# One common set of four PSUM banks for scores and transposes, in place of two private pairs, in a two-layer decoder trunk

## The chip, the core and the metric

The kernel runs on one core of a Trainium2 chip. The metric is the device time of one execution in microseconds (us), the median of several runs. Five engines work side by side, each through its own queue in order: TensorE (PE, matmuls and transposes; PEld is its weight load), VectorE (DVE), ScalarE (ACT), GpSimd (POOL) and SyncE (SP), which issues most DMA transfers. PE writes its results to PSUM, eight banks of 128 partitions by 512 fp32 values; DVE and ACT read them out from there.

## The reference, cut to what matters

x is 512 tokens by 1024 features, fp32. Layer 0 mixes tokens by stick-breaking heads and differential heads, layer 1 by dilated heads; each layer then has a squared-ReLU MLP (1024 to 4096 and back) and a gated embedding.

```python
for i in range(DEPTH):                       # DEPTH = 2
    hn = rmsnorm(h, norm_mix_g[i])
    h = h + (even_mixer if i % 2 == 0 else odd_mixer)(hn, ...)
    hn = rmsnorm(h, norm_mlp_g[i])
    u = square(relu(hn @ w_mlp_up[i]))
    h = h + u @ w_mlp_down[i]
    gate = sigmoid(rmsnorm(h, norm_ple_g[i]) @ w_ple_gate[i])
    h = h + (p[i] @ w_ple_proj[i]) * gate
return rmsnorm(h, final_norm_g)

# differential heads:  prob = softmax(scale * q.k + bias);  attn = prob[0] - lam * prob[1];  o = attn @ v
# stick-breaking:      z = scale * q.k;  w = exp(log_sigmoid(z) + sum of log_keep over later keys);  o = w @ v
# dilated:             three causal branches (window, stride), combined by their softmax denominators
```

## The kernel before, in words

**Precision.** Every fp32 operand of a large matmul is split into a high part (`hi`, `wh`, `uh`, by an ACT copy, L119 for weights, L168 for activations) and a low part (`lo`, `wl`, `ul`, by a subtraction, L120 on DVE or POOL for weights, L169 on DVE). A product is three matmuls: L128, L129 and L130 in the trace.

**Stages.** A layer is: statistics of its norm, the mixer with its projections, the output projection, the MLP, the gate. In the mixer the heads are taken in four groups; layer 0 takes groups 2 and 3 (differential) and then 0 and 1 (stick-breaking), layer 1 four dilated groups. `project` makes values, queries and keys of one group; while it runs for group g+1, `attend` handles group g, in steps interleaved with it. A step computes the scores of one 128-token block (L460, L461), lets DVE and ACT make weights of them (L475 and L478, L479 for softmax; L536, L539 for stick-breaking), and three steps later transposes the weights on PE (L486), after which ACT and DVE copy them out as a high and a low part (L490, L491); two steps later they multiply the values (L501).

**Norm.** `finish` sums squares over partitions with two matmuls (L236, L237); rsqrt on ACT and DVE follows (L192 to L198). `tok_cols` transposes the result into token columns with four transposes (L259), which wait for the last DVE step, L198; L261 reads them out, and the evacuation of values (L397, L398) needs them. `prepare` (layer 0 alone) makes the bias rows with two small matmuls (L315) and reads them out on DVE (L317).

**The last gate.** `ple_final` makes the gate token by token: eight groups of four transposes of the stream h (L707), each copied out by DVE (L708), beside the split of the gate's weights (L119, L120) and the gate's matmuls.

**PSUM.** `ps(tag)` draws a bank of a tag. Before, there are three banks "mm" for projection accumulators, two "sc" for scores (and `prepare`), two "tp" for transposes (and for norm sums, `tok_cols` and `ple_final`) and one "pv". `ps_wide` walks round all eight for wide stages: the projection of a layer's first group, the MLP, the gate.

**What sets the order.** The kernel is written in a framework whose scheduler orders each engine's instructions by the data they need and the engines' queues. One rule of it matters here, as the orders below show it: the tiles of one tag get their banks in the order of the program, that is, of each tile's first writer. A tile of one tag can be started ahead of an earlier tile of another tag, never ahead of one of its own. A tile's first writer waits until the reader of the tile that held the bank before has read it.

Of the kernel before, what the change touches and what calls it, by code (L numbers as in the profile page):

```python
# [61 lines left out]
def trunk(  # L62
# [8 lines left out]
    def nm(s):  # L71
        uid[0] += 1
        return f"{s}_{uid[0]}"
# [8 lines left out]
    def const(shape, name, dtype=F32):  # L82
        return cpool.tile(shape, dtype, tag=name, name=name)
# [3 lines left out]
    def t2k(tag, pool=None, dtype=F32):  # L87
        return (pool or spool).tile([P, S], dtype, tag=tag, name=nm(tag), bufs=T_BUFS.get(tag, 2))
# [1 line left out]
    def col(name="c"):  # L90
        return spool.tile([P, 1], F32, tag="col", name=nm(name), bufs=24)

    PS_BUFS = {"mm": 3, "sc": 2, "tp": 2, "pv": 1}

    def ps(tag):
        return psum.tile([P, S], F32, tag=tag, name=nm(tag), bufs=PS_BUFS[tag])

    wide = ["mm", "mm", "mm", "sc", "sc", "tp", "tp", "pv"]
    wide_i = [0]

    def ps_wide():
# [89 lines left out]
    def rsqrt(y, t, mean, eps, eps_t, scale=1.0, tables=None):  # L191
        ln = nc.scalar.activation(y, mean, AF.Ln, bias=eps_t, scale=scale)  # L192
        if tables is not None:
            order(ln.ins, tables)
        nc.scalar.activation(y, y, AF.Exp, scale=-0.5)
        nc.vector.tensor_tensor(t, y, y, op=ALU.mult)
        nc.vector.scalar_tensor_tensor(t, mean, eps / scale, t, op0=ALU.add, op1=ALU.mult)
        nc.vector.scalar_tensor_tensor(y, t, 3.0 / scale, y, op0=ALU.subtract, op1=ALU.mult)  # L198
# [13 lines left out]
    class Norm:  # L212
# [16 lines left out]
                nc.vector.tensor_tensor(self.acc, self.acc, sq, op=ALU.add)  # L229

        def finish(self, tables=None):
            mp = ps("tp")
            hi, lo = t2k("e", dtype=F32R), t2k("e", dtype=F32R)
            nc.scalar.activation(hi, self.acc, AF.Copy)
            nc.vector.tensor_tensor(lo, self.acc, hi.bitcast(F32), op=ALU.subtract)
            nc.tensor.matmul(mp, ones_r, hi, start=True, stop=False)  # L236
            nc.tensor.matmul(mp, ones_r, lo, start=False, stop=True)  # L237
            rsqrt(self.acc, t2k("e"), mp, NORM_EPS, eps_n, tables=tables)
            return self.acc
# [14 lines left out]
            newton(dst, x, t)  # L254

    def tok_cols(rstd):
        rp = ps("tp")
        for t in range(QT):
            nc.tensor.transpose(rp[:, t * P:(t + 1) * P], rstd[:, t * P:(t + 1) * P], ident)  # L259
        rc = spool.tile([P, QT], F32, tag="rcol", name=nm("rcol"), bufs=2)  # L260
        nc.vector.tensor_scalar(rc, rp.rearrange("p (t c) -> p t c", c=P)[:, :, 0], -0.5, None, op0=ALU.mult)  # L261
        return rc
# [37 lines left out]
    def prepare():  # L300
        a, b, c, d = (t2k("e") for _ in range(4))
        lamt = t2k("tmp")[:, 0:4 * HD].rearrange("p (j c) -> p j c", j=4)
        nc.sync.dma_start(d[0:32, 384:400], t5_table)
        nc.sync.dma_start(a[0:32], onehot[:, 0:512])
        nc.sync.dma_start(d[0:32, 0:128], onehot[:, 512:640])
        for l, m in enumerate((b, c)):
            nc.sync.dma_start(m[0:16], bass.AP(tensor=offs.tensor, offset=offs.offset + l * UL, ap=[[0, 16], [1, 512]]))
        nc.sync.dma_start(
            d[0:16, 128:384].rearrange("p (l c) -> p l c", l=2),
            bass.AP(tensor=offs.tensor, offset=offs.offset + 512, ap=[[0, 16], [UL, 2], [1, 128]]))  # L310
        nc.sync.dma_start(lamt, bass.AP(tensor=lambdas.tensor, offset=lambdas.offset, ap=[[0, P], [HD, 4], [1, HD]]))
        for c0, src, offm in ((0, a[0:32], (b[0:16], c[0:16])),
                              (512, d[0:32, 0:128], (d[0:16, 128:256], d[0:16, 256:384]))):
            up = ps("sc")[0:16, 0:src.shape[-1]]
            nc.tensor.matmul(up, d[0:32, 384:400], src, start=True, stop=True)  # L315
            for l in range(2):
                nc.vector.scalar_tensor_tensor(offm[l], up, -1.0, offm[l], op0=ALU.mult, op1=ALU.add)  # L317
                nc.sync.dma_start(urow[l, :, c0:c0 + src.shape[-1]], offm[l])
        nc.vector.tensor_tensor(lamt[:, 0:2, :], lamt[:, 0:2, :], lamt[:, 2:4, :], op=ALU.mult)
        lsum = const([P, 2], "lsum")  # L320
        nc.vector.reduce_sum(lsum, lamt[:, 0:2, :], axis=AX.X)
        nc.scalar.activation(lsum, lsum, AF.Exp)
        nc.vector.tensor_tensor(neglam, lsum[:, 1:2], lsum[:, 0:1], op=ALU.subtract)
        nc.vector.tensor_scalar(neglam, neglam, -LAMBDA_INIT, None, op0=ALU.add)
        nc.vector.tensor_scalar(gsub, gcols[:, 48:49], -0.5 * (D // P) * (1.0 - LAMBDA_INIT), None, op0=ALU.mult)
# [10 lines left out]
    def mixer(layer, norm, nxt):  # L336
        st = ExitStack()
# [11 lines left out]
        def statistics():  # L349
            if not layer:  # L350
                for k in range(KT):
                    norm.stats(k, last_split)
            stat["rstd"] = norm.finish(use_tables(sig_tail) if layer else None)
            stat["rcol"] = tok_cols(stat["rstd"])
# [100 lines left out]
        def scores(hd, i):  # L455
            q, kh, kl = hd
            n = max(256, P * (i + 1))
            sp = ps("sc")
            qs = slice(i * P, (i + 1) * P)
            nc.tensor.matmul(sp[:, 0:n], q[:, qs], kh[:, 0:n], start=True, stop=False)  # L460
            nc.tensor.matmul(sp[:, 0:n], q[:, qs], kl[:, 0:n], start=False, stop=True)  # L461
            return sp
# [18 lines left out]

        def transpose_in(e, i, pt):
            n = P * (i + 1)
            tp = ps("tp")
            for j in range(i + 1):
                nc.tensor.transpose(tp[:, j * P:(j + 1) * P], e[:, j * P:(j + 1) * P], ident)  # L486
            src = tp[:, 0:n].rearrange("p (j c) -> p j c", c=P)
            dh = pth[pt][:, i:i + 3 * i + 1:3, :]
            dl = ptl[pt][:, i:i + 3 * i + 1:3, :]
            nc.scalar.activation(dh, src, AF.Copy)  # L490
            nc.vector.tensor_tensor(dl, src, dh.bitcast(F32), op=ALU.subtract)  # L491
# [13 lines left out]
        def attend(g, kind, v, heads):  # L505
# [66 lines left out]
            def step(n):  # L572
                if n < QT * nh:
                    ready[n] = weights(n // QT, n % QT)
                m = n - LAG
                if 0 <= m < QT * nh:
                    transpose_in(ready.pop(m), m % QT, pts[m // QT])
                m = n - LAG - PVLAG
                if m >= 0 and m % QT == QT - 1 and m // QT < nh:
                    combine(m // QT)  # L580
                m -= 1
                if kind == "diff" and m >= 0 and m % QT == QT - 1 and m // QT < nh:
                    subnorm(m // QT)
# [17 lines left out]
        if layer == 0:  # L601
            prepare()
# [94 lines left out]
    def ple_final(layer, fpool, pj, norm):  # L697
# [4 lines left out]
        for t in range(QT):  # L702
            ht = fpool.tile([P, D], F32, tag=f"ht{t}", name=nm("ht"), bufs=1)
            for c in range(2):
                tp = ps("tp")
                for k in range(4):
                    nc.tensor.transpose(tp[:, k * P:(k + 1) * P], h[4 * c + k][:, t * P:(t + 1) * P], ident)  # L707
                nc.vector.tensor_copy(ht[:, 512 * c:512 * c + 512], tp)  # L708
            hk.append(ht)
# [13 lines left out]
        for c in range(2):  # L723
# [17 lines left out]
            if c == 0:  # L741
                for b in range(4):
                    for t in range(QT):
                        contract(t, b, 0)
                    if b == 1:
                        rcol = tok_cols(norm.finish())
            for t in range(QT):
# [28 lines left out]
                if t < QT - 2:  # L776
                    finish(*done.pop())
        for t, r in done[::-1]:
            finish(t, r, () if t == QT - 1 else (ex, ad))

    sig_tail = []
    for layer in range(DEPTH):
        n_mlp, n_ple, n_next = Norm(1, layer), Norm(2, layer), Norm(0, layer + 1)
        mixer(layer, norm, n_mlp)
        with tc.tile_pool(name=f"ppool{layer}", bufs=1) as ppool:
            lo_eng[0] = nc.vector
            pj = ple_proj(layer, ppool)
            with tc.tile_pool(name=f"fpool{layer}", bufs=1) as fpool:
                mlp(layer, fpool, n_mlp, n_ple)
            with tc.tile_pool(name=f"gpool{layer}", bufs=1) as gpool:  # L790
                if layer < DEPTH - 1:
                    ple_t(layer, gpool, pj, n_ple, n_next)
                else:
                    ple_final(layer, gpool, pj, n_ple)
        norm = n_next
        lo_eng[0] = nc.gpsimd
# [77 lines left out]
```

## Time and profile before

| | |
|---|---|
| median of 3 runs | 1342.75 us (1341.68 to 1342.84) |
| the profiled execution | 1343.02 us |
| its span in the trace | 1341.2 us, so 1.8 us lie around it |
| instructions | 16293 |
| PE, matmuls on it | 6360 |
| mean granted clock of PE | 0.995 |
| PE idle for L259 to get the norm's result | 3.1 us in two places |

The profile gives busy time per engine, idle time before an instruction and what ended it. A timeline row is: start (us), duration (us), engine, line, operation, out<-in, shape, count; in brackets, when there was idle time ahead of it, how long and what ended it. Matmuls overlap, so a duration is longer than the step to the next: the wide matmuls (512 columns) follow each other at some 0.23 us although each row says 0.39. A window row gives the busy time of the engines in that stretch, then the granted clock of PE (1.00 is full) and the share and rate of the DMA. The prediction shows the rows it uses.

### The profile page before, as it was taken

What the parts mean: (1) busy time and instruction counts of PE and PEld (TensorE: products, weight loads), DVE (VectorE), ACT (ScalarE), POOL (GpSimd) and SP (SyncE); (2) the same over time, 40 slices, a digit from 0 to 9 for tenths busy, and PEclk for the clock granted to TensorE, in tenths of its full rate; (3) what the DMA queues carried; (4) which work ended last, traced back from release to release, by engine and by line L of the source; (5) the groups of instructions that cost most, each with busy time, mean ns of one, the idle gap of its engine ahead of it and who ended that gap; (6) DMA issues with size and microseconds to landing.
All of it is one profiled execution on the core that took longest, in us unless ns stands there. A gap on an engine that the chain in (4) does not pass through costs nothing.

```text
span 1341.2 us, 16293 instructions
## 1 busy us (share of the span) xinstructions
PE 1302.9 (97%) x6360; PEld 1090.5 (81%) x6360; DVE 818.1 (61%) x1397; ACT 633.2 (47%) x1087; POOL 149.0 (11%) x84
## 2 busy tenths in 40 slices
PE   8999988999999999999999999999999999999997
PEld 6878876788888888888879889788888888888886
DVE  6688899765344343445767888977544434434566
ACT  6576766564233232344456667766422313224334
POOL 2222322200000000000013222221000000000001
PEclk9999999999999999999999999999999999999999
DMA  6322101322222223222232222223222222232221
GB/s 218 101 95 70 56 26 48 111 86 103 94 95 94 96 100 106 104 99 94 94 118 79 79 87 79 64 95 110 94 95 95 94 97 100 104 106 96 95 79 64
DMA packets 23453, 124.66 MB, mean 93 GB/s; under 512 B 2832, under 2 KB 3568, under 8 KB 10704
## 3 DMA queue, kind: packets, MB, share of 16 engines
q1 hardware_dynamic: 23376, 123.62, 26.9%
q8 instruction: 50, 0.82, 0.2%
q14 instruction: 27, 0.22, 0.1%
HBM read 121.43 MB, written 2.18 MB: 92 GB/s over the span
## 4 chain that ended last, share of the span: by engine, by line
PE 77%; DVE 14%; ACT 6%; issue 2%; DMA 0%; SPq 0%; ACTq 0%
PE mm L129 12%; PE mm L128 12%; PE mm L130 12%; PE tp L130 5%; PE tp L129 5%; PE tp L128 5%; PE sc L130 5%; PE sc L129 5%; PE sc L128 5%; PE pv L129 3%; PE pv L130 3%; PE pv L128 3%; DVE qq L434 2%; PE pv L501 2%; DVE e L539 1%
## 5 line engine op out<-in xcount | busy, mean ns | idle before, releaser
L119 ACT ACTIVATE wh<-raw 128x1024 fp32r<-128x1024 f32 (+1 forms) x214 | 222.4, 1042 | 504.3 <-PE mm L129 176.9
L128 PE MATMUL mm<-hi,wh 128*128 128x512 f32 x564 | 226.3, 401 | 1.4 <-ACT wh L294 1.3
L120 DVE TENSOR_TENSOR wl<-raw,wh 128x1024 fp32r<-128x1024 f32 x154 | 188.1, 1224 | 59.6 <-ACT wh L119 35.9
L129 PE MATMUL mm<-lo,wh 128*128 128x512 f32 x564 | 220.8, 391 | 0.4 <-DVE lo L169 0.4
L130 PE MATMUL mm<-hi,wl 128*128 128x512 f32 x564 | 220.6, 391 | 0.3 <-DVE wl L120 0.3
L120 POOL TENSOR_TENSOR wl<-raw,wh 128x1024 fp32r<-128x1024 f32 (+1 forms) x60 | 138.3, 2306 | 347.6 <-ACT wh L119 326.2
L130 PEld LDWEIGHTS mm<-hi,wl 128*128 128x128 f32 x564 | 105.9, 188 | 23.2 <-DVE wl L120 0.7
L128 PEld LDWEIGHTS mm<-hi,wh 128*128 128x128 f32 x564 | 106.1, 188 | 21.8 <-ACT wh L294 1.5
L129 PEld LDWEIGHTS mm<-lo,wh 128*128 128x128 f32 x564 | 106.2, 188 | 20.3 <-DVE lo L169 1.1
L478 ACT ACTIVATE e<-e,mn 128x128 f32<-128x128 f32 (+3 forms) x96 | 53.9, 561 | 51.1 <-DVE mn L475 50.6
L128 PE MATMUL mm<-uh,wh 128*128 128x512 f32 x192 | 74.7, 389 | 0.0
L129 PE MATMUL mm<-ul,wh 128*128 128x512 f32 x192 | 74.7, 389 | 0.0
L130 PE MATMUL mm<-uh,wl 128*128 128x512 f32 x192 | 74.7, 389 | 0.0
L130 PE MATMUL sc<-hi,wl 128*128 128x512 f32 x168 | 66.3, 395 | 0.0
L129 PE MATMUL sc<-lo,wh 128*128 128x512 f32 x168 | 65.9, 392 | 0.0
L128 PE MATMUL sc<-hi,wh 128*128 128x512 f32 x168 | 65.8, 392 | 0.0
L128 PE MATMUL mm<-wh,hi 128*128 128x256 f32 (+1 forms) x216 | 65.8, 305 | 0.0
L129 PE MATMUL mm<-wl,hi 128*128 128x256 f32 (+1 forms) x216 | 64.7, 300 | 0.4 <-DVE wl L120 0.4
L130 PE MATMUL mm<-wh,lo 128*128 128x256 f32 (+1 forms) x216 | 64.3, 298 | 0.0
L645 DVE TENSOR_TENSOR h<-h,mm 128x512 f32<-128x512 f32 x24 | 16.5, 687 | 72.7 <-PE mm L130 72.7
L129 PE MATMUL tp<-lo,wh 128*128 128x512 f32 x152 | 59.1, 389 | 0.0
L128 PE MATMUL tp<-hi,wh 128*128 128x512 f32 x152 | 59.1, 389 | 0.0
(265 smaller groups left out, 2837.1 us busy)
## 6 DMA issues: line engine op xcount, KB each, us to landing
raw<-in_w_up_dram SPq DMA_DIRECT2D x32, 1024.0 KB, 4.9
raw<-in_w_down_dram SPq DMA_DIRECT2D x32, 1024.0 KB, 4.9
raw<-in_w_in_dram SPq DMA_DIRECT2D x23, 1024.0 KB, 4.9
raw<-in_w_gate_dram SPq DMA_DIRECT2D x8, 1024.0 KB, 4.8
bias<-urow SPq DMA_DIRECT2D x24, 256.0 KB, 3.2
raw<-in_w_outa_dram SPq DMA_DIRECT2D x8, 768.0 KB, 4.3
h<-in_xT_dram SPq DMA_DIRECT2D x8, 256.0 KB, 5.5
raw<-in_w_outb_dram SPq DMA_DIRECT2D x2, 1024.0 KB, 4.8
```

Source lines behind the costliest of these rows:

```text
L119: nc.scalar.activation(hi, src, AF.Copy)
L120: lo_eng[0].tensor_tensor(lo, src, hi.bitcast(F32), op=ALU.subtract)
L128: nc.tensor.matmul(acc, lh, rh, start=start, stop=False)
L129: nc.tensor.matmul(acc, lh, rl, start=False, stop=False)
L130: nc.tensor.matmul(acc, ll, rh, start=False, stop=stop)
L434: nc.vector.tensor_tensor(q[b], f[a], q[a].bitcast(F32), op=ALU.subtract)
L478: nc.scalar.activation(e[:, 0:n], e[:, 0:n], AF.Exp, scale=-1.0, bias=mn, accum_out=s)
L501: nc.tensor.matmul(op[:, q0:S], stat(j), mov, start=c == 0, stop=c == nmm - 1)
L539: nc.vector.tensor_tensor_scan(kr, kr, kr, 1.0, op0=ALU.mult, op1=ALU.bypass)
L645: nc.vector.tensor_tensor(h[2 * c + i], h[2 * c + i], acc, op=ALU.add)
```

## The change

The tags "sc" and "tp" become one tag, "st", with four banks. The number of banks stays eight, nothing is computed otherwise, and the round of `ps_wide` names the new tag in the same four places. Every tile that was of a pair, of the scores, transposes, norm sums, `tok_cols`, `prepare` and `ple_final`, takes its bank from the common four, in program order.

```diff
-    PS_BUFS = {"mm": 3, "sc": 2, "tp": 2, "pv": 1}
+    PS_BUFS = {"mm": 3, "st": 4, "pv": 1}
...
-    wide = ["mm", "mm", "mm", "sc", "sc", "tp", "tp", "pv"]
+    wide = ["mm", "mm", "mm", "st", "st", "st", "st", "pv"]
...
         def finish(self, tables=None):
-            mp = ps("tp")
+            mp = ps("st")
...
     def tok_cols(rstd):
-        rp = ps("tp")
+        rp = ps("st")
...
-            up = ps("sc")[0:16, 0:src.shape[-1]]
+            up = ps("st")[0:16, 0:src.shape[-1]]
...
-            sp = ps("sc")
+            sp = ps("st")
...
         def transpose_in(e, i, pt):
             n = P * (i + 1)
-            tp = ps("tp")
+            tp = ps("st")
...
             for c in range(2):
-                tp = ps("tp")
+                tp = ps("st")
```

Three places show what the scheduler makes of it. The first is on PE at the start of layer 0: L236 and L237 sum the norm, `sc_264` (now `st_264`) is an accumulator of the second half of the keys, L259 are `tok_cols`' four transposes. Before:

```order
L236 MATMUL tp_312<-e_313,ones_r 128x512
L237 MATMUL tp_312<-e_314,ones_r 128x512
L128 MATMUL sc_264<-hi_130,wh_259 128x512
...
L128 MATMUL sc_264<-hi_162,wh_259 128x512
L129 MATMUL sc_264<-lo_163,wh_259 128x512
L259 MATMUL tp_325<-ident,rstd_289 128x128 x4
L130 MATMUL sc_264<-hi_162,wl_260 128x512
L128 MATMUL sc_264<-hi_166,wh_259 128x512
```

Of the change:

```order
L236 MATMUL st_312<-e_313,ones_r 128x512
L237 MATMUL st_312<-e_314,ones_r 128x512
L259 MATMUL st_325<-ident,rstd_289 128x128 x4
L128 MATMUL st_264<-hi_130,wh_259 128x512
L129 MATMUL st_264<-lo_131,wh_259 128x512
L130 MATMUL st_264<-hi_130,wl_260 128x512
```

Before, 17 matmuls of the key accumulator (L128 to L129) stood between L237 and L259; now L259 comes straight behind L237, and all of the accumulator behind it. In program order the accumulator's first writer comes after `tok_cols`. The start of layer 1 shows the same move.

The second place is on PE, in the first group's attention (differential): scores of two heads (L460, L461, `kh_1028` and `kh_1032`) among the projection of the next group (`mm_1103`, `mm_1104`). Before:

```order
L130 MATMUL mm_1103<-wh_1105,lo_151 128x256
L460 MATMUL sc_1159<-kh_1028,qq_878 128x256
L461 MATMUL sc_1159<-klz_175,qq_878 128x256
L128 MATMUL mm_1104<-wh_1105,hi_130 128x256
L129 MATMUL mm_1104<-wl_1106,hi_130 128x256
...
L128 MATMUL mm_1104<-wh_1105,hi_130 128x256
L460 MATMUL sc_1169<-kh_1032,qq_881 128x256
L461 MATMUL sc_1169<-klz_177,qq_881 128x256
L129 MATMUL mm_1104<-wl_1106,hi_130 128x256
```

Of the change:

```order
L130 MATMUL mm_1103<-wh_1105,lo_151 128x256
L460 MATMUL st_1159<-kh_1028,qq_878 128x256
L461 MATMUL st_1159<-klz_175,qq_878 128x256
L460 MATMUL st_1169<-kh_1032,qq_881 128x256
L461 MATMUL st_1169<-klz_177,qq_881 128x256
L128 MATMUL mm_1104<-wh_1105,hi_130 128x256
L129 MATMUL mm_1104<-wl_1106,hi_130 128x256
L130 MATMUL mm_1104<-wh_1105,lo_131 128x256
```

Before, 13 matmuls of `mm_1104` stood between the two heads' scores; now the second follows the first directly. (The same holds for the next pair.)

The third place is on DVE at the last gate: L645 ends the MLP, L708 copies a transposed tile out, L120 makes the low part of the gate's weights. Before:

```order
L645 TENSOR_TENSOR h_97<-h_97,tp_10648 128x512
L708 COPY ht_10687<-tp_10688 128x512
L120 TENSOR_TENSOR wl_10746<-raw_10743,wh_10745 128x1024
L169 SCALAR_TENSOR_TENSOR lo_10675<-h_97,gcols,hi_10674 128x512
L229 TENSOR_TENSOR rstd_10418<-rstd_10418,e_10678 128x512
L708 COPY ht_10687<-tp_10694 128x512
L708 COPY ht_10700<-tp_10701 128x512
L120 TENSOR_TENSOR wl_10750<-raw_10743,wh_10749 128x1024
L708 COPY ht_10700<-tp_10707 128x512
```

Of the change:

```order
L645 TENSOR_TENSOR h_97<-h_97,st_10648 128x512
L708 COPY ht_10687<-st_10688 128x512
L708 COPY ht_10687<-st_10694 128x512
L169 SCALAR_TENSOR_TENSOR lo_10675<-h_97,gcols,hi_10674 128x512
L229 TENSOR_TENSOR rstd_10418<-rstd_10418,e_10678 128x512
L708 COPY ht_10700<-st_10701 128x512
L708 COPY ht_10700<-st_10707 128x512
L708 COPY ht_10713<-st_10714 128x512
L708 COPY ht_10713<-st_10720 128x512
L708 COPY ht_10726<-st_10727 128x512
L708 COPY ht_10726<-st_10733 128x512
L120 TENSOR_TENSOR wl_10746<-raw_10743,wh_10745 128x1024
```

Before, L120 alternated with the copies of the transposed stream, the first of them behind one copy; now all eight copies stand first. On PE, in the same way, the eight groups of L707 transposes stand ahead of nearly all of the gate's matmuls, with only four L128 among and behind them before the first one that needs a low part. L236 of the norm stands behind the last of these four, L237 behind the 44 matmuls that follow.

Elsewhere ACT's copies L119 move by a place or a few among the exps, one weight load on SP (L111) moves behind the load of the lambdas (L311), POOL's order is the same, and in the attention scores and transposes move by a few rows against the projection's matmuls.

## The prediction

> **What bounds the kernel now.** The busy row of the page and its shares of the chain come first.
>
> ```profile
> PE 1302.9 (97%) x6360; PEld 1090.5 (81%) x6360; DVE 818.1 (61%) x1397; ACT 633.2 (47%) x1087; POOL 149.0 (11%) x84
> PE 77%; DVE 14%; ACT 6%; issue 2%; DMA 0%; SPq 0%; ACTq 0%
> ```
>
> TensorE (PE) is busy 97% of a span of 1341.2 us; 38.3 us are idle, the most that shorter waits could bring at an unchanged clock. The chain gives VectorE (DVE) 14%, so somewhere DVE sets the pace. Windows by stage (times; then busy us of PE, PEld, DVE, ACT, POOL; granted clock; DMA) show where:
>
> ```profile
> 150.00:260.00 110.00, 97.49 (x530) 79.82 (x531) 99.34 (x173) 70.93 (x149) 28.20 (x13) 1.00 0.15 50
> 260.00:695.00 435.00, 435.00 (x1920) 360.04 (x1920) 217.06 (x265) 165.92 (x219) 5.46 (x6) 1.00 0.29 100
> 714.30:870.00 155.70, 151.94 (x920) 133.82 (x918) 132.96 (x322) 106.67 (x240) 44.25 (x20) 1.00 0.26 84
> 870.00:1282.00 412.00, 411.98 (x1853) 341.96 (x1852) 201.32 (x288) 155.33 (x230) 14.36 (x7) 1.00 0.28 96
> ```
>
> From 260 to 695 and from 870 to 1282 PE never rests: whatever it is late at 260 or 870 it is late at the end. In the stick-breaking attention (150 to 260) DVE is busy 99.34 of 110 us, PE 97.49: DVE and its exchange with ScalarE (ACT) set the pace. The waits of PE (total us, times, longest):
>
> ```profile
> PE sc L460 <- ACT e L536: 7.8, 9, 1.8
> PE tp L486 <- DVE ptl L491: 5.9, 6, 2.2
> PE sc L460 <- DVE mn L475: 5.0, 4, 1.8
> PE tp L259 <- DVE rstd L198: 3.1, 2, 2.0
> ```
>
> The first three wait for a bank of a private pair; the change can touch them. The fourth waits for data; more banks don't help it.
>
> **Part A, start of layer 0.** The order shows the four L259 transposes moved ahead of 17 matmuls.
>
> ```profile
> 25.35 0.40 PE L237 MATMUL tp<-e,ones_r 128*128 128x512 f32 x1
> 25.59 0.40 PE L128 MATMUL sc<-hi,wh 128*128 128x512 f32 x1
> ...
> 29.27 0.39 PE L129 MATMUL sc<-lo,wh 128*128 128x512 f32 x1
> 31.63 0.94 PE L259 MATMUL tp<-ident,rstd 128*128 128x128 f32 x4 [1.98 <-DVE rstd L198]
> 30.89 0.69 DVE L198 SCALAR_TENSOR_TENSOR rstd<-e,rstd 128x512 f32<-128x512 f32 x1
> 31.86:35.27 3.41, 3.41 (x11) 2.84 (x10) 2.67 (x5) 1.35 (x3) 0.00 (x0) 0.50 0.73 272
> 49.76 0.39 PE L315 MATMUL sc<-e 32*16 32x128 f32 x2 [1.81 <-DVE v L398]
> ```
>
> L259 needs rstd, done at 31.58 (30.89 + 0.69). The chain to it starts from L237, which stands where it stood, so L259 still starts at 31.63. The 17 matmuls at 25.59 to 29.27 (16 steps in 3.68 us, 0.23 each) filled that time; now they follow it: 17 x 0.23 = 3.9 us later, PE idle 25.8 to 31.6. The window row shows a half clock from 31.86 after the 1.98 us; the same window stays. L315's second tile waited 1.81 us for a bank; it now has a free one, which gives that back: 3.9 - 1.8 = **+2.1 us** into the attention. Behind the waiting L259 on PE stand those 17 and then the values' projection, for which DVE and ACT wait; that is the loss counted. The rest of the move is on SP:
>
> ```profile
> 46.92 0.35 SPq L111 DMA_DIRECT2D raw<-in_w_in_dram  x1
> 48.23 0.35 SPq L311 DMA_DIRECT2D tmp<-in_lambdas_dram  x1
> 56.64 1.06 ACT L119 ACTIVATE wh<-raw 128x1024 fp32r<-128x1024 f32 x1 [2.97 <-PE mm L130]
> ```
>
> The weight load L111 falls behind the lambda load L311, so about 1.6 us later. The split that reads it began 9.7 us after the issue and had idled 2.97 us until PE released it, which covers 1.6: 0 (up to 1.6 without that cover).
>
> [...]
>
> **Part B, differential attention (99 to 120).**
>
> ```profile
> 106.61 0.39 PE L460 MATMUL sc<-kh,qq 128*128 128x256 f32 x1 [1.84 <-DVE mn L475]
> 106.95:110.37 3.42, 3.42 (x17) 3.42 (x16) 1.78 (x9) 0.87 (x5) 0.00 (x0) 0.50 0.00 0
> 110.24 1.06 ACT L119 ACTIVATE wh<-raw 128x1024 fp32r<-128x1024 f32 x1 [1.98 <-PE mm L130]
> 111.83 0.17 DVE L479 RECIPROCAL r<-s 128x1 f32<-128x1 f32 x1 [3.04 <-ACT e L478]
> 115.04 0.50 PE L460 MATMUL sc<-kh,qq 128*128 128x512 f32 x1 [0.96 <-DVE mn L475]
> ```
>
> The score tile at 106.61 waited 1.84 us for one of two banks; then the clock was at half for 3.42 us, half of it lost (1.7); another score waited 0.96. With four banks both heads' scores go in a pair ahead of the projection's matmuls, as the order shows, so PE could win 1.84 + 1.7 + 0.96 = 4.5. DVE bounds that: its largest hole is 3.04 us, waiting for an exp that stood on ACT behind L119, which itself waited 1.98 for PE; L119 now stands behind the second 256-wide exp. I take the hole: **-3.0** (ends -4.5 and 0, if the data come no sooner).
>
> **Part C, stick-breaking attention.** A common four gives a score its bank when the fourth tile before it, scores and transposes alternating, is read out; that is the same distance as two scores back. With DVE at 99.34 of 110 us the waits for L536 and L491 return in another place. The ends are 0 and minus DVE's idle time, 10.7; the order keeps alternating nearly everywhere, so near 0: **-0.3**.
>
> **Part D, start of layer 1.** The same move.
>
> ```profile
> 695.46 0.40 PE L128 MATMUL sc<-hi,wh 128*128 128x512 f32 x1
> ...
> 699.13 0.39 PE L129 MATMUL sc<-lo,wh 128*128 128x512 f32 x1
> 700.65 0.66 PE L259 MATMUL tp<-ident,rstd 128*128 128x128 f32 x4 [1.13 <-DVE rstd L198]
> 695.45:704.00 8.55, 7.42 (x40) 6.04 (x39) 5.96 (x8) 4.14 (x6) 2.47 (x2) 1.00 0.36 126
> PE tp L486 <- DVE ptl L491: 1.4, 2, 0.7
> PE sc L460 <- DVE mn L475: 1.3, 1, 1.3
> PE sc L460 <- DVE v L398: 1.0, 1, 1.0
> ```
>
> Again 17 matmuls (695.46 to 699.13) fall behind L259: +3.9. Before, 1.13 us idle left the clock at 1.00; now PE is idle 695.5 to 700.65, 5.2 us, so I add a half clock: 3.41 / 2 = 1.7 (ends 0 and 2.5, one and a half windows). PE now comes later to the attention, and lateness swallows waits: the last three rows (of a window from 690 to 880) hold 1.4 + 1.3 + 1.0 = 3.7, and each stall costs some 0.15 more than listed (29.27 to 31.63 is 2.36, less one matmul 2.13, listed 1.98), about 0.9 for six (the three rows count four; two are below the list). 3.9 + 1.7 - 4.6 = **+1.0**.
>
> **Part E, the last gate.** The order has all eight L708 copies on DVE ahead of the first L120 (the low half of the gate's weights); one stood there before.
>
> ```profile
> 1283.20 0.68 DVE L708 COPY ht<-tp 128x512 f32<-128x512 f32 x1
> 1283.80 1.21 DVE L120 TENSOR_TENSOR wl<-raw,wh 128x1024 fp32r<-128x1024 f32 x1
> 1284.93 0.74 DVE L169 SCALAR_TENSOR_TENSOR lo<-h,gcols,hi 128x512 fp32r<-128x512 f32 x1
> 1285.59 0.68 DVE L229 TENSOR_TENSOR rstd<-rstd,e 128x512 f32<-128x512 f32 x1
> 1286.20 1.28 DVE L708 COPY ht<-tp 128x512 f32<-128x512 f32 x2
> 1285.07 0.50 PE L129 MATMUL pv<-wl,hi 128*128 128x512 f32 x1
> 1297.82 0.39 PE L236 MATMUL tp<-e,ones_r 128*128 128x512 f32 x1
> 1316.40 0.50 PE L129 MATMUL mm<-wl,hi 128*128 128x512 f32 x1 [0.41 <-DVE wl L120]
> ```
>
> From 1283.80 DVE does seven copies (0.60 each by the x2 row's step), L169 (0.66) and L229 (0.61), 5.5 us, then L120 (1.15): the first wl is ready near 1290.5; before, its L120 began at 1283.80 and the L129 that needs it ran at 1285.07. PE has only transposes, four L128 and L236 ahead of its first L129, so it waits from about 1286 to 1290.6. Behind that stand 44 matmuls up to L237: 44 x 0.233 = 10.25, so L237 at 1300.85. Before, it stood behind L236, a step of 0.23 after 1297.82, at 1298.05: +2.8. The norm's chain and the gate's scaling hang on L237, so nothing later hides it. [...] The wait of 0.41 at 1316.40 is swallowed: **+4.1** (ends +2.4 without half clock, +5.3).
>
> [...]
>
> **Sum.** A +2.1, B -3.0, C -0.3, D +1.0, E +4.1: +3.9 on the profiled run's 1343.02, 1346.9. The median of the runs lies 0.27 below that run: **1346.7**.
>
> **Rivals.** (1) *The attention keeps what four banks win* (ends faster). Mechanism: bank waits were what held DVE in layer 0, in places where the score stood behind its own private pair; once scores run two ahead, DVE fills its idle 10.7 us of 150 to 260. It speaks for it that 7.8 + 5.9 + 5.0 us are listed as bank waits; against it that DVE is at 90%. It decides once C reaches -7: then the sum is -2.8, 1340. (2) *The shifts are absorbed* (no change): no new half clock in D and E (-3.4, because 1.13 us left the clock alone), sum +0.5: about 1343.5. (3) *Pooling displaces a wait*: a transpose queues behind a score tile that DVE has not read, in both attention stages; each of the 6 L486 waits recurring at its longest, 2.2, beside the old ones, adds up to 6 us: about 1351. (4) *The order doesn't change*, then 1342.8; the order's rows show that it does.
>
> **How the numbers follow.** Forecast 0.56, (1) 0.13, (2) 0.18, (3) 0.12, (4) 0.01. About 0.2% (2.7 us) is what a measurement of this kernel can tell from no change. Faster is (1) less its weak half, 0.11; same is (2), (4), and the low end of the forecast where B gives its 4.5, 0.25; slower is the rest, 0.64. The range runs from B and C at their gains with one half clock missing (+3.9 - 1.5 - 2 - 1.7 = -1.3) to B giving nothing (+3.0) and a third of (3) (+2), +8.9; from the median 1342.75 that is 1341.4 to 1351.6.
>
> **What would show it.** A: L259 right behind L237, PE idle 25.8 to 31.6. B: no wait at the score near 106, no clock of 0.5 in the 22 us after 99, DVE's 3 us hole gone. D: 5.2 us idle before L259 near 698, half a clock after it, fewer waits to 880. E: the first L129 of the last gate five us after the first L128, half a clock from there. The forecast is wrong if PE reaches 260 more than 4 us ahead of before (rival 1), or the windows after the idle times of D and E show a clock of 1.00 (rival 2).

## The result, and the profile after

The changed kernel takes 1357.49 us (median of 5 runs, 1356.52 to 1357.73) against 1342.84 for the kernel before: ratio 1.0108, 95% interval 1.0098 to 1.0119. It is slower by 14.65 us; the forecast was slower by 3.9, with a range that ended at 1351.6. The sign was right, the size was not. The profiled execution took 1356.52 us with a span of 1354.7, 13.5 longer than before's.

The busy row on the page of the changed kernel:

```profile
PE 1307.8 (97%) x6360; PEld 1094.1 (81%) x6360; DVE 818.8 (60%) x1397; ACT 632.1 (47%) x1087; POOL 148.1 (11%) x84
```

Its waits of PE (us in total, times, longest):

```profile
PE st L259 <- DVE rstd L198: 10.8, 2, 5.8
PE st L486 <- DVE ptl L491: 4.6, 5, 2.4
PE st L460 <- DVE mn L475: 2.9, 3, 1.5
PE pv L567 <- ACT tmp L564: 2.9, 2, 2.2
PE st L460 <- DVE ptl L491: 2.9, 2, 1.8
PE st L460 <- ACT e L536: 1.9, 2, 1.7
```

PE does the same work; its 4.9 us more of busy time go with more half clock (20.4 us in the rows below, up to 1304 us, against 6.8 before). L259's waits grew from 3.1 to 10.8; the bank waits of the scores shrank (L460 on L536 from 7.8 to 1.9, on L475 from 5.0 to 2.9), but L567 and other pairs of tiles wait that did not before, and scores now wait for VectorE's reading of transposes (L460 on L491).

Where the time went is read from the start of the same instruction in both traces, matched by its line and its count among that line's instructions: the difference is how late PE is. Where the order has changed, the matched instruction can stand behind a few rows more or less, which is worth some tenths of a us. Rows of the timeline before:

```profile
51.48 0.28 PE L130 MATMUL mm<-wh,lo 128*128 128x256 f32 x1
149.91 0.50 PE L568 MATMUL pv<-tmp,ones_r 128*128 128x512 f32 x1 [0.23 <-DVE tmp L565]
694.98 0.40 PE L236 MATMUL tp<-e,ones_r 128*128 128x512 f32 x1
711.99 0.28 PE L130 MATMUL tp<-wh,lo 128*128 128x256 f32 x1
874.93 0.47 PE L128 MATMUL mm<-hi,wh 128*128 128x512 f32 x1
1282.16 0.40 PE L130 MATMUL tp<-uh,wl 128*128 128x512 f32 x1
```

The same instructions in the changed kernel, and ahead of them and behind them L237, which is at 25.35 and 1298.05 (1297.82 + 0.23) before:

```profile
24.86 0.39 PE L237 MATMUL st<-e,ones_r 128*128 128x512 f32 x1
53.09 0.28 PE L130 MATMUL mm<-wh,lo 128*128 128x256 f32 x1
155.01 0.50 PE L568 MATMUL pv<-tmp,ones_r 128*128 128x512 f32 x1 [0.22 <-DVE tmp L565]
700.46 0.40 PE L236 MATMUL st<-e,ones_r 128*128 128x512 f32 x1
723.10 0.28 PE L130 MATMUL st<-wh,lo 128*128 128x256 f32 x1
884.04 0.48 PE L128 MATMUL mm<-hi,wh 128*128 128x512 f32 x1
1291.25 0.40 PE L130 MATMUL st<-uh,wl 128*128 128x512 f32 x1
1311.47 0.39 PE L237 MATMUL st<-e,ones_r 128*128 128x512 f32 x1
```

| part | lateness from, to (us) | measured | forecast |
|---|---|---|---|
| A, start of layer 0 | -0.49 to +1.61 | +2.1 | +2.1 |
| B, differential groups | +1.61 to +5.10 | **+3.5** | -3.0 |
| C, stick-breaking groups | +5.10 to +5.48 | +0.4 | -0.3 |
| D, start of layer 1 | +5.48 to +11.11 | +5.6 | +5.6 |
| D, waits regained in layer 1 | +11.11 to +9.11 | **-2.0** | -4.6 |
| E, last gate | +9.09 to +13.42 | +4.3 | +4.1 |

The parts sum to 13.9, and 13.4 with the -0.5 of the lead-in. A, the first half of D, and E came out as worked out; B failed by 6.5 us, the second half of D by 2.6. The rows of A, D and E in the changed kernel's timeline of PE:

```profile
31.04 1.11 PE L259 MATMUL st<-ident,rstd 128*128 128x128 f32 x4 [5.79 <-DVE rstd L198]
706.07 0.90 PE L259 MATMUL st<-ident,rstd 128*128 128x128 f32 x3 [4.98 <-DVE rstd L198]
876.31 0.50 PE L128 MATMUL mm<-hi,wh 128*128 128x512 f32 x1 [0.81 <-ACT hi L165]
877.42 0.50 PE L129 MATMUL mm<-lo,wh 128*128 128x512 f32 x1 [0.61 <-DVE lo L166]
1299.61 0.50 PE L129 MATMUL st<-wl,hi 128*128 128x512 f32 x1 [1.77 <-DVE wl L120]
```

The stretches of half clock in the changed kernel up to 1304 us (the granted clock is the third number from the end):

```profile
27.30:34.11 6.81, 3.07 (x10) 2.58 (x11) 6.11 (x8) 1.26 (x2) 1.69 (x1) 0.50 0.72 257
102.40:105.80 3.40, 3.18 (x11) 2.69 (x11) 0.96 (x2) 2.03 (x3) 0.21 (x1) 0.50 0.00 0
703.13:709.95 6.82, 3.88 (x11) 3.23 (x12) 5.73 (x8) 1.61 (x3) 0.88 (x1) 0.50 0.44 154
1300.50:1303.90 3.40, 3.40 (x10) 2.63 (x9) 3.06 (x4) 0.00 (x0) 0.00 (x0) 0.50 0.63 200
```

And DVE at the last gate:

```profile
1294.75 3.67 DVE L708 COPY ht<-st 128x512 f32<-128x512 f32 x6
1298.34 4.62 DVE L120 TENSOR_TENSOR wl<-raw,wh 128x1024 fp32r<-128x1024 f32 x4
```

The 17 matmuls' time is idle time ahead of L259 at both starts; the half clock at both starts begins while PE is still idle and lasts 6.8 us, of which PE works 3.1 and 3.9; another, of 3.4 us, follows the idle time of the last gate, 1.77 us ahead of L129; and the first L120 of the last gate stands behind the copies, its consumer at 1299.61, which is 1290.5 plus the lateness of 9.1. The two rows near 876 show what became of the waits of layer 1: some are gone, but the next stage now waits for the output heads (L165, L166).

### The profile page after: what moved, and what is told of

It is laid out like the page before. It is cut to its first block, busy times and chain, and to the rows that moved or that the text cites. A ratio compares the mean times of both kernels' runs of the same rounds, so it can differ in the third digit from the quotient of the medians.

```text
span 1354.7 us, 16288 instructions
## 1 busy us (share of the span) xinstructions
PE 1307.8 (97%) x6360; PEld 1094.1 (81%) x6360; DVE 818.8 (60%) x1397; ACT 632.1 (47%) x1087; POOL 148.1 (11%) x84
## 4 chain that ended last, share of the span: by engine, by line
PE 77%; DVE 15%; ACT 5%; issue 2%; DMA 1%; SPq 0%; ACTq 0%
PE mm L129 11%; PE mm L128 11%; PE mm L130 11%; PE st L129 11%; PE st L130 11%; PE st L128 11%; PE pv L130 3%; PE pv L129 3%; PE pv L128 3%; DVE qq L434 2%; DVE e L539 1%; PE pv L501 1%; DVE e L540 1%; DVE e L475 1%; DVE ptl L491 1%
## 5 line engine op out<-in xcount | busy, mean ns | idle before, releaser
L119 ACT ACTIVATE wh<-raw 128x1024 fp32r<-128x1024 f32 (+1 forms) x214 | 222.4, 1042 | 508.6 <-PE st L129 218.6
L128 PE MATMUL mm<-hi,wh 128*128 128x512 f32 x564 | 227.2, 403 | 2.0 <-ACT hi L165 1.9
L120 DVE TENSOR_TENSOR wl<-raw,wh 128x1024 fp32r<-128x1024 f32 x154 | 187.8, 1224 | 64.2 <-ACT wh L119 40.5
L129 PE MATMUL mm<-lo,wh 128*128 128x512 f32 x564 | 221.3, 392 | 1.7 <-DVE lo L166 1.4
L120 POOL TENSOR_TENSOR wl<-raw,wh 128x1024 fp32r<-128x1024 f32 (+1 forms) x60 | 137.5, 2291 | 357.6 <-ACT wh L119 345.8
L128 PE MATMUL st<-hi,wh 128*128 128x512 f32 x320 | 126.0, 394 | 0.0
L129 PE MATMUL st<-lo,wh 128*128 128x512 f32 x320 | 125.4, 392 | 0.0
L130 PE MATMUL st<-hi,wl 128*128 128x512 f32 x320 | 125.3, 391 | 0.0
L128 PEld LDWEIGHTS mm<-hi,wh 128*128 128x128 f32 x564 | 106.3, 189 | 23.1 <-ACT hi L165 2.8
L129 PEld LDWEIGHTS mm<-lo,wh 128*128 128x128 f32 x564 | 106.5, 189 | 21.4 <-DVE lo L166 2.0
L130 PE MATMUL st<-uh,wl 128*128 128x512 f32 x256 | 99.6, 389 | 0.0
L129 PE MATMUL st<-ul,wh 128*128 128x512 f32 x256 | 99.6, 389 | 0.0
L128 PE MATMUL st<-uh,wh 128*128 128x512 f32 x256 | 99.6, 389 | 0.0
L645 DVE TENSOR_TENSOR h<-h,st 128x512 f32<-128x512 f32 x32 | 22.0, 687 | 95.2 <-PE st L130 95.2
L128 PE MATMUL mm<-uh,wh 128*128 128x512 f32 x192 | 74.7, 389 | 0.0
L129 PE MATMUL mm<-ul,wh 128*128 128x512 f32 x192 | 74.7, 389 | 0.0
L633 DVE SCALAR_TENSOR_TENSOR u<-st,rstd 128x512 f32<-128x512 f32 x32 | 22.1, 691 | 84.8 <-PE st L130 84.7
L129 PEld LDWEIGHTS st<-lo,wh 128*128 128x128 f32 x320 | 60.8, 190 | 12.7
```

The costliest lines, as they stand in the source:

```text
L119: nc.scalar.activation(hi, src, AF.Copy)
L120: lo_eng[0].tensor_tensor(lo, src, hi.bitcast(F32), op=ALU.subtract)
L128: nc.tensor.matmul(acc, lh, rh, start=start, stop=False)
L129: nc.tensor.matmul(acc, lh, rl, start=False, stop=False)
L130: nc.tensor.matmul(acc, ll, rh, start=False, stop=stop)
L633: nc.vector.scalar_tensor_tensor(u, acc, 0.0, rstd, op0=ALU.max, op1=ALU.mult)
```

## The experiments

The lateness of PE against before, in us, at the same instructions, in each profiled run (the table's columns are the times of before), with the median of the runs and the ratio to before:

| run | 51 | 150 | 695 | 712 | 875 | 1298 | median | ratio, 95% interval |
|---|---|---|---|---|---|---|---|---|
| the change | 1.6 | 5.1 | 5.5 | 11.1 | 9.1 | 13.4 | 1357.49 | 1.0108 (1.0098, 1.0119) |
| e1 | -0.9 | 1.9 | 2.3 | 2.3 | 0.3 | 3.1 | 1348.58 | 1.0041 (1.0027, 1.0055) |
| e2 | 1.7 | 5.2 | 5.6 | 11.2 | 9.2 | 8.4 | 1352.35 | 1.0068 (1.0053, 1.0083) |
| e3 | -0.2 | 3.0 | 3.4 | 3.4 | 1.4 | 0.7 | 1343.50 | 1.0000 (0.9991, 1.0009) |
| e4 | 1.7 | 8.4 | 9.7 | 12.1 | 9.7 | 14.1 | 1354.40 | 1.0083 (1.0063, 1.0104) |
| e5 | -1.2 | 1.6 | 2.0 | 2.0 | -0.1 | -0.9 | 1343.19 | 1.0001 (0.9992, 1.0010) |
| e6 | 0.2 | 0.1 | 0.2 | 0.2 | -1.9 | -2.6 | 1339.92 | 0.9973 (0.9962, 0.9983) |
| e7 | -0.2 | 6.6 | 6.9 | 6.9 | 5.0 | 4.2 | 1347.27 | 1.0033 (1.0020, 1.0045) |
| e8 | -0.8 | 3.3 | 5.1 | 5.1 | 3.1 | 2.3 | 1345.08 | 1.0015 (1.0005, 1.0024) |
| e9 | 0.1 | 0.7 | 1.8 | 1.8 | -0.2 | -0.9 | 1341.31 | 0.9991 (0.9981, 1.0000) |

The first column carries up to 1.7 us of chance, half of 3.4: whether a half clock follows the idle time near 30 us differs between the profiled runs (the granted clock from 32 to 34 us is 0.50 before and 0.53 in e6, 1.00 in e1, e3 and e9). So the differences between columns are read, not the columns alone. The later steps hold half clocks too: from 51 to 260 us there are 3.4 us of it before and in the change, less than 1 in e1 and e3, but 17 to 18 in e4, e8 and e9.

### e1: the start undone

```diff
-    def tok_cols(rstd):
-        rp = ps("st")
+    def tok_cols(rstd, tag="st"):
+        rp = ps(tag)
...
-            stat["rcol"] = tok_cols(stat["rstd"])
+            stat["rcol"] = tok_cols(stat["rstd"], "pv")
```

> The change with one tile taken out of the common set: in the mixers, tok_cols draws the bank of pv, so L259 stands behind 17 matmuls of the key accumulator again at the start of both layers; the attention keeps its order. Theory carry (the loss of layer 0 between 60 and 140 us is the 2 us of lateness from the start, carried and enlarged by VectorE): with the start undone PE reaches 260 us at +1 to +2 instead of +5.5, layer 1 gains 3.6 to 5.6 at its start and loses again what lateness absorbed there; about 1350 us. Rival order (the scores' own new order in the differential groups costs 3 us whatever comes before): PE reaches 260 at +4 to +5.5, only layer 1 gains, about 1354 us.

1348.58 us, 8.9 less than the change (10.3 in the profiled runs). In the lateness, 5.6 of it comes at the start of layer 1 (2.3 stays 2.3) and 2.5 at the one of layer 0. The last gate gives 1.5 more, although its order is the one of the change: e1's profiled run has no half clock there (1.00 from 1283 to 1294 us), and without it the gate costs 2.8 and not 4.3. But between 51 and 150 the attention still loses 2.8. So PE reaches 260 at +2.3 between the two theories' numbers, and by its step the rival is right: the loss of the differential groups does not come from lateness carried in.

### e2: the last gate undone

```diff
                 nc.vector.tensor_copy(ht[:, 512 * c:512 * c + 512], tp)
+                if c == 0:
+                    if t % 2 == 0:
+                        raws.append(wload(w_gate[layer, t // 2]))
+                    gw0.append(wsplit(raws[-1], t % 2, 2, 512, pool=fpool))
...
-            gw = []
-            for half in range(2):
+            gw = list(gw0) if c == 0 else []
+            for half in range(2) if c else ():
```

> The change with the weight splits of the last gate written between the copies of the transposed stream, so that VectorE has the order of before there (one copy, L120, ..., copies and L120 by turns). All else as in the change. Theory tail (+4.4 us of the loss is PE waiting for the first low half at the last gate, and nothing later hides it): 1357.5 - 4.4 = 1353.1 us, a lag of PE against before of about +9.1 up to the end. Rival (the end waits for VectorE's other work, so the gain is lost again before the end): over 1355.5 us.

1352.35 us, 5.1 less than the change: the 4.4 and a little more, since with four banks and this order the gate is 0.8 faster than before's (9.2 to 8.4). The order of DVE at the gate is the whole of part E.

### e3: both

> Both of these together: what is left of the change is the common set in prepare, the norm's sums, scores and transposes. Theory carry: 1350 - 4.4 = about 1345.5 us, near before plus 3. Rival order: 1354 - 4.4 = about 1349.5 us, before plus 7. If the four banks themselves gain once the start and the tail are as before: under 1342.

1343.50 us, the time of before. That is no absence of effect but a sum: +3.1 from 51 to 150, +0.4 to 695, -2.0 in layer 1, -0.7 at the gate. The waits of PE from 55 to 150 us, before and in e3, show the +3.1:

```profile
PE sc L460 <- DVE mn L475: 3.7, 3, 1.8
PE tp L486 <- DVE e L521: 0.9, 1, 0.9
PE pv L568 <- DVE tmp L565: 0.2, 1, 0.2
```

```profile
PE st L460 <- DVE mn L475: 3.4, 4, 1.5
PE pv L567 <- ACT tmp L564: 2.9, 2, 2.2
PE st L486 <- DVE mn L475: 1.2, 2, 0.7
PE pv L568 <- DVE tmp L565: 0.5, 2, 0.2
```

4.8 us before, 8.0 in e3. The waits that I had expected to go did go at their places (near 106 and 115); others of the same kind came in new places, and L567 and L486 wait where they had not. And the equal medians flatter e3: in its profiled run no half clock stands where the kernel before has one, from 106.95 (mean clock from 56 to 160 us 1.00, 0.98 before), and its ten runs have mean clocks of 0.993 to 0.999, before's fourteen beside them 0.990 to 0.997.

### e4: four tags of one bank

```diff
+        if tag == "st":
+            st_i[0] += 1
+            tag = f"st{st_i[0] % 4}"
```

> The change with four tags of one bank each, drawn by turns: the same four banks in the same round, but tiles of different banks may be started out of the order of the program. L259 falls back behind the 17 matmuls by itself, the last gate keeps all eight copies first, the scores of the differential groups stand in another order again. Theory order of the program (the loss at both starts comes from one order for all tiles, not from the sharing): layer 1's start costs nothing, the tail still costs 4.4, so 1350 to 1352 us. Rival sharing (the four banks in common cost in the attention whatever the order): 1354 us or more.

1354.40 us, on the rival's side, though for parts of both; the four runs go from 1351.56 to 1357.12, and the profiled one is the slowest. L259 waits 3.2 us as before, yet layer 1's start costs 2.4 in another way: an accumulator of the values, whose bank is now fixed by its turn, waits 0.9 for L427's reading of the bank (and 1.4 at the start of layer 0), and a score waits 0.7. The gate costs 4.4 as expected, and the attention loses 6.7 from 51 to 150, of which up to 1.7 is one half clock more than before. Freeing the order but keeping the round does not help.

### e5: one weight split earlier

The added ordering edge makes the scheduler put L119 four places earlier on ACT; all else is e3.

```diff
                     wh, wl = wsplit(raw, half, 4, 256)
+                    if g == 0 and not layer and half == 0:
+                        order(qq_act[-2], wh_act[-1])
```

> Start and tail restored as in e3, and one ACT instruction put back where the kernel before has it: the high-half split L119 of the third group's values stands ahead of the query copies L433, four places earlier, so that GpSimd's L120 behind it starts near 85 us and not at 89. Theory collision (GpSimd's L120 holds VectorE up for its 2.4 us; in e3 two of them, at 89 and 92, fall on L196 and L198, on which the waits of 2.16 us at L567 near 100 hang): the wait at L567 goes, PE's lag near 104 falls from +2.7 to +0.7, the lag at 260 from +3.4 to +1.5 to +2.5; 1 to 2 us faster than e3. Rival (VectorE has as much to do wherever the split stands): lag at 260 within 0.5 of +3.4, the time of e3.

1343.19 us, the time of e3, and the theory falls. GpSimd's two splits now start at 85.28 and 91.06, the wait at L567 stays (2.22), and the step from 51 to 150 is 2.8. The lag at 260 is +2.0, within the theory's numbers, but only because PE was already 1.0 earlier than in e3 at 51. The first split held up another instruction instead (the line numbers of e5 are 3 higher; L437 is the query split L434):

```profile
85.90 2.77 DVE L437 TENSOR_TENSOR qq<-tmp,qq 64x512 fp32r<-64x512 f32 x1
```

### e6: common banks in layer 1 and at the last gate alone

```diff
+    def ps_st(own, common):
+        if not common:
+            return ps(own)
+        st_i[0] += 1
+        return ps(("tp", "sc")[st_i[0] % 2])
...
-            sp = ps("sc")
+            sp = ps_st("sc", layer)
...
-            tp = ps("tp")
+            tp = ps_st("tp", layer)
```

With the edit of e2 at the gate, its tile drawn by `ps_st("tp", True)`.

> The kernel before in layer 0 and at both starts; in layer 1's attention scores and transposes draw the two pairs by turns, so four banks in one round; the last gate's tile too, with the weight splits between the copies as in e2. PE's order in layer 1 is that of before. Theory free banks (the 2.0 us that PE regains in layer 1, 715 to 870, come from banks that are free sooner, not from arriving late): -2.0 there and -0.9 in the tail, 2.9 us faster than before, ratio 0.998. Rival lateness (only a PE that comes late finds the waits gone): -0.9, ratio 0.9993.

1339.92 us, the fastest kernel of this study: 3.7 less than the 1343.65 of before in the same set of runs, 2.6 by the lateness, where 2.9 was expected. Layer 1 regains 2.0 although PE arrives only 0.2 late, so these 2.0 us are banks that come free sooner: PE, VectorE, ScalarE and GpSimd have the order of before in that stretch. PE's waits from 690 to 880 in e6 (its lines are 7 higher: L135, L136 are L128, L129, and L172, L173 are L165, L166):

```profile
PE tp L266 <- DVE rstd L205: 1.1, 1, 1.1
PE mm L135 <- ACT hi L172: 0.8, 1, 0.8
PE mm L136 <- DVE lo L173: 0.6, 1, 0.6
PE pv L508 <- DVE ptl L498: 0.5, 2, 0.3
```

The three bank waits of 3.7 us before are gone, and 1.9 us of waits for data have taken their place. The changed kernel, 11 us late, has the same rows near 876: lateness swallows nothing more.

### e7: transposes written ahead of scores

```diff
                 m = n - LAG
+                early = kind == "diff"
+                if early and 0 <= m < QT * nh:
+                    transpose_in(ready.pop(m), m % QT, pts[m // QT])
                 if n < QT * nh:
                     ready[n] = weights(n // QT, n % QT)
-                m = n - LAG
-                if 0 <= m < QT * nh:
+                if not early and 0 <= m < QT * nh:
```

> e3 with the two halves of a step of the differential groups exchanged in the program: the transposes of the block three steps back are written ahead of the scores of this step, so that in the common round they get their banks first. Theory order of the round (in the kernel before the transposes ran ahead of scores written earlier; one common round holds them behind these scores, and VectorE and ACT get the blocks of the weights later): the loss of 3.4 us in layer 0 falls to 1 or less at 260 us, 2 us faster than e3. Rival (the loss is where GpSimd's splits fall, whatever the order of scores and transposes): the lag at 260 stays between +2.5 and +4.5.

Slower, 1347.27 us. Up to 130 us the theory holds: PE is at -0.3 there (e3: +1.8), and the first readings of transposes by VectorE are back at their times of before (before, e3, e7):

```profile
61.42 0.28 DVE L491 TENSOR_TENSOR ptl<-tp,pth 128x128 fp32r<-128x128 f32 x1
64.74 0.42 DVE L491 TENSOR_TENSOR ptl<-tp,pth 128x256 fp32r<-128x256 f32 x1 [0.53 <-ACT pth L490]
```

```profile
64.41 0.28 DVE L491 TENSOR_TENSOR ptl<-st,pth 128x128 fp32r<-128x128 f32 x1
70.01 0.41 DVE L491 TENSOR_TENSOR ptl<-st,pth 128x256 fp32r<-128x256 f32 x1
```

```profile
61.16 0.28 DVE L491 TENSOR_TENSOR ptl<-st,pth 128x128 fp32r<-128x128 f32 x1
64.41 0.42 DVE L491 TENSOR_TENSOR ptl<-st,pth 128x256 fp32r<-128x256 f32 x1 [0.45 <-ACT pth L490]
```

Then it falls, and not by the banks of the scores: PE computes the last two scores of the second group at 127.71 and 128.25, earlier than before (128.00 and 128.46). VectorE reads the last but one 4.9 us later than before, because in its queue L520, L434 twice, L521 and a reading of a transpose now stand ahead (before, e7):

```profile
128.66 0.69 DVE L475 CUSTOM_DVE_ANT_0 e<-sc,bias 128x512 f32<-128x512 f32 x1
133.57 0.68 DVE L475 CUSTOM_DVE_ANT_0 e<-st,bias 128x512 f32<-128x512 f32 x1
```

At the end of the group L567 waits 2.8 and L568 1.5, the latter for L565, which takes 2.44 us beside a split of GpSimd (0.69 before); the clock is at half from 141.3 to 148.2. So e7 shows that the order of the round made the first transposes late. It does not show that scores written second come late for their banks.

### e8: the sub-norm ahead of the key copies

```diff
+                hi_act = nc.scalar.activation(hi, rs, AF.Copy).ins
+                if x == 1:
+                    order(kh_act[-2], hi_act)
```

> e3 (the change with start and tail restored) with one group of ACT instructions moved in both differential groups: the three that feed the second sub-norm (L550, L563, L564) stand ahead of the four key copies L441 and L442, not behind them. Theory queue (the three wait in ACT's queue behind key copies that wait for VectorE's L427, so PE waits 2.16 us at L567 near 100 and 0.69 near 139, the first with half a clock behind it): these waits go, PE's lag against before near 100 falls from +2.7 to +0.5 or less, at 260 from +3.4 to +1 or less, 2 us and more faster than e3. Rival (VectorE's work sets the pace of both groups: key copies that come 1.9 us later make the next scores wait): the wait at L567 goes, the scores wait instead, lag at 260 between +2.5 and +4.5.

1345.08 us, and the theory falls. In the trace of the first group the three stand ahead of three of the four key copies; the first wait at L567 shrank to 0.4, and PE was at +0.4 near 100. But the scores waited more (L460 on L475 4.0 us from 55 to 150), the second group's L567 waited 1.5, and PE reaches 695 at +5.1, beyond the rival's numbers too. Part of these 5.1 is the clock: five half clocks lie between 116 and 247 us, none in e3. The fastest of the ten runs, with a mean clock of 0.997, took 1343.81, so even so nothing is gained over e3. The wait at L567 was where the lateness showed, not its cause.

### e9: stick-breaking groups too

```diff
-            sp = ps_st("sc", layer)
+            sp = ps_st("sc", turns[0])
...
             def step(n):
+                turns[0] = kind != "diff"
```

> e6 with the stick-breaking groups of layer 0 drawing the two pairs by turns as well; only the differential groups keep private pairs. Theory of the prediction's part C, measured in the change as a lag of +0.3 from 160 to 260: +0.3, so 1339.9 + 0.3 = 1340.2 us. Rival (waits of 7.8 us for the exchange with ScalarE are bank waits that four banks end): 2 us or more faster than e6.

1341.31 us, 1.4 more than e6; from 150 to 695 PE loses 1.1. The 1.1 can't be read as a price of the banks: e9's profiled run has three half clocks between 184 and 243 us, e6 and the change none, and the change, with its common four, loses 0.4 there. Four banks bring the stick-breaking groups nothing, as part C had it. From 51 to 150, where the differential groups have private pairs, PE's order is that of before, and it loses 0.6 (with 7.0 us of half clock for 3.4 before) where e3 loses 3.1.

## Why the prediction was right in its sign and wrong in its size

**Right: the program order of one tag.** Parts A and D (start) and E, 12.0 of the 13.9 us by the lateness, are what tiles of one tag lose when a tile written late in the program (the key accumulator; the gate's accumulator) can't be started ahead of one written earlier that waits for data (L259, the L707 groups). e1 and e2 give back 8.9 and 5.1 us. The half clocks of D and E came at about their price (in A and D the clock is at half for 6.8 us, twice as long as forecast, but the first part of it falls into PE's idle time), and the one of E with some luck: e1, with the same order at the gate, has none there. The end that the prediction gave for that case, +2.4, is near the 2.8 measured. No run shows how long an idle time must be for a half clock to follow, so the 1.7 in E's +4.1 was an assumption: the longest wait of PE at the gate is 1.77 us in the changed kernel, with 3.4 us of half clock after it, and 1.8 in e1, with a clock of 1.00 after it.

**Wrong: part B, -3.0 forecast, +3.5 measured.** The step that failed is to price the differential groups by "With four banks both heads' scores go in a pair ahead of the projection's matmuls, as the order shows, so PE could win 1.84 + 1.7 + 0.96 = 4.5", and to put at nothing what the same move does to the transposes. The 4.5 came, and VectorE's hole of 3.04 did not bound it: from 104 to 116 us the lateness falls from +5.9 to +0.8 in the change (from +3.0 to -1.5 in e3), and VectorE's longest hole there is 0.7. But the change lost 4.3 ahead of it, from 51 to 104, and 4.3 behind it, from 116 to 150. The half clock, too, was not gone but came earlier, from 102.40, behind a wait of 2.2 at L567.

What the step left out is the second kind of tile in the same round: it can be held by the scores' reading on VectorE (L486 on L475, 1.2 us in e3), and its place is behind them. In e3 PE makes the first two groups of transposes at 62.91 and 66.25, 2.2 and 2.4 us later than before (60.71 and 63.90), and VectorE reads them 3.0 and 5.3 us late (the rows of e7's section). The weights, the products and the sub-norm follow. I had it as rival (3), at 0.12, but for both attention stages and on top of the gain; its price of 6 does not follow from its own terms either, since six waits of 2.2 are 13.2. e3 shows the loss with the start undone, e9 its absence with private pairs in these groups, and e7 that with the transposes first their delay goes.

The record shows a second path to the same loss, which no experiment separates from the first. Where VectorE takes longer than usual in these groups, a split of GpSimd runs beside it (near 91 us in the changed kernel L196 takes 2.48 us beside one, 0.69 at its median), and with the new times and order it meets the splits less luckily. The column "VectorE held up" adds up what VectorE's instructions from 51 to 150 us took beyond the median of the same line and shape in all traces, where that is over 0.25 us; every one of them overlaps a split. All columns are in us.

| run | PE loses, 51 to 150 | VectorE held up | half clock in the stretch |
|---|---|---|---|
| before | 0 | 11.3 | 3.4 |
| e6 | -0.1 | 11.3 | 3.4 |
| e9 | 0.6 | 11.2 | 7.0 |
| the change | 3.5 | 14.6 | 3.4 |
| e1 | 2.8 | 14.6 | 0 |
| e2 | 3.4 | 14.5 | 3.4 |
| e3 | 3.1 | 14.6 | 0.7 |
| e5 | 2.8 | 14.9 | 0 |
| e8 | 4.1 | 14.7 | 7.7 |
| e4 | 6.7 | 15.2 | 6.8 |
| e7 | 6.8 | 17.1 | 6.8 |

Every run that loses 2.8 us or more here has VectorE held up by at least 3.2 us more than before, and neither of the others. So the loss may be in good part an accident of where the splits fall (the last section shows 0.61 and 2.70 us for one instruction, with starts that differ by 0.2 us against the split) and not the price of the banks. e5 moved one split, and it fell on another instruction; e8 shows that the place of the sub-norm in ScalarE's queue isn't the cause. How the 3 us divide stays open: no run kept the splits off VectorE with the round in common.

**Wrong: the second half of D, -4.6 forecast, -2.0 measured.** "Lateness swallows waits" was the wrong reason: e6 regains the same 2.0 with PE on time. And the sum of listed waits overstated the gain, since 1.4 us came back near 876 as waits for data that had stood behind the bank waits; of the 0.9 added for what a stall costs beyond its listing, 0.2 came (PE's idle time there fell by 1.8).

**Right: part C**, near nothing, at 0.4 for -0.3. In this stage, with VectorE about 90% busy in both kernels, the bank waits came back elsewhere: L460 on L536 fell from 7.8 to 1.9, the waits on L491 rose from 4.4 to 7.5, and PE is idle 13.5 us there, 12.5 before. The stage in the changed kernel:

```profile
155.10:265.48 110.38, 96.88 (x530) 79.92 (x531) 100.12 (x173) 70.63 (x149) 28.34 (x13) 1.00 0.14 50
```

Rival (1), the faster side, is out: it wanted -7 there.

## What to carry to other kernels

Before pooling buffers, list the kinds of tile that will share them and ask which waits for data: in one round in program order a tile can wait for a slower kind ahead of it, and an accumulator that filled idle time may no longer start. Where the order of the engines stayed (layer 1), the common banks were worth 2.0 us; where the order moved, it cost 2 to 6 at each place, so compare the orders first and price the moved rows. A listed bank wait is not yet its gain: look for the wait for data that stands right behind it (layer 1 gave 2.0 of 3.7), and for the half clock that may go with it. Ask, too, which instructions the new order puts beside GpSimd's work.

## What the runs showed of the hardware

One VectorE instruction beside GpSimd's weight split took 0.61 us before and 2.70 in the changed kernel. Before, L521 starts 0.08 us ahead of the split, and it is the split that takes longer, 2.79 instead of 2.40. In the changed kernel the split starts 0.11 us ahead, and L521 takes 2.70 (before, then the changed kernel):

```profile
66.80 0.61 DVE L521 SCALAR_TENSOR_TENSOR e<-e,r,e 128x384 f32<-128x384 f32 x1
66.88 2.79 POOL L120 TENSOR_TENSOR wl<-raw,wh 128x1024 fp32r<-128x1024 f32 x1 [6.69 <-ACT wh L119]
```

```profile
68.19 2.70 DVE L521 SCALAR_TENSOR_TENSOR e<-e,r,e 128x384 f32<-128x384 f32 x1
68.08 2.40 POOL L120 TENSOR_TENSOR wl<-raw,wh 128x1024 fp32r<-128x1024 f32 x1 [6.29 <-ACT wh L119]
```

In the changed kernel L521 ends 0.4 us after the split does. The order of the starts does not decide it alone: at 115.34 us of the changed kernel L521 (128x256) starts 0.01 us ahead of the split and takes 2.69 (0.48 at 126.68 before).

The idle time of a gap did not by itself decide on a half clock. The 1.98 us ahead of L259 near 31 us brought one before (0.50 from 31.86 to 35.27), and 2.01 us at the same place none in e3, whose clock there is 1.00 and which has one near 50:

```profile
30.00:36.00 6.00, 4.02 (x28) 3.73 (x29) 4.78 (x8) 2.81 (x4) 0.81 (x1) 1.00 0.63 202
48.00:53.00 5.00, 4.38 (x24) 4.38 (x25) 4.30 (x11) 1.93 (x5) 2.37 (x1) 0.66 0.54 208
```

By estimate 3.4 us of work at a clock of 0.50 lose half of that, 1.7 us, so this alone moves these kernels against each other. The mean clock differs between runs of one kernel too: of the 21 runs of before in the last set, those with a mean clock of 0.997 took 1340.26 to 1340.92 us, those with 0.991 took 1343.67 to 1344.27. The stretches of half clock that are quoted are 3.4 us long, or twice that (6.8 at both starts of the changed kernel).
